# A two-layer diffusion trunk on one core: the end of shared products, the queue of the modulation loads, and buffers for S5's tiles

## The chip, the cores and the metric
One of the eight cores of a Trainium2 chip runs the whole program in one launch. The metric is device time in microseconds (us). Engines: TensorE (PE: matrix products; PEld is its weight load), VectorE (DVE), ScalarE (ACT), GpSimd (POOL) and SyncE (SP). SP issues most DMA transfers, POOL some. Each engine runs its own list of instructions in order and waits on semaphores.

## The reference
Two layers (`DEPTH` 2) over 512 latent tokens and 256 context tokens of width 1024, all in float32:

```
mod = silu(c) @ w_mod[l] + b_mod[l]          # 6 x 1024 values per stream: shift, scale, gate, twice
h   = rmsnorm(x) * (1 + scale) + shift       # latent with c, context with c_ctx
y   = token_mixing(h @ w_in[l])              # S5 | neighbourhood attention | gated linear attention | windowed attention
x   = x + gate * rmsnorm(y @ w_out[l])
h   = rmsnorm(x) * (1 + scale2) + shift2
x   = x + gate2 * rmsnorm((gelu(conv3(h @ w_up_gate)) * (h @ w_up_val)) @ w_down[l])
```

In the last layer the context stream is not updated after the input projection. The output is the latent stream.

## The kernel before
Activations lie with channels on the partitions: H is eight tiles (k = 0 to 7) of 128 channels x 768 tokens, each split into a high part h and a remainder l. Weights are split too: `weights` (line 448) loads 128 x 1024 floats into `wst` (2 buffers) on SP's queue, ACT casts them to `whi`, DVE subtracts to get `wlo` (`split`, lines 268 and 269; four buffers each). A product is then three matmuls: whi x h, whi x l, wlo x h.

`dense4` (line 506) forms several output tiles at once, four of them or six, with four or six weights held. It walks the quarters of tokens (context 512 to 767, then 0 to 255, then 256 to 511), in a quarter the eight k, and for each k all tiles j. It is called four times: at the start of layer 0 (`start`, with the k in two halves), for the first four tiles of layer 1's input projection (`mixing`), and at the start of each layer's FFN (`ffn_start`; four tiles in layer 0, six in layer 1). Its tiles hold the PSUM buffers with the tags m (four) and d (two). After it come single products: `dense` (line 468) in the FFN, `dense_steps` (line 479) in the projections.

Work that can run beside others is written as Python generators: `tails` (the ends of rows: norm, residual, transposes L412, next input L285), `fill` (projections that fill PE's time), `later` (modulation). `step_tail` advances the tails; `gap` advances `fill` by one step, the tails by two, and `later` by `rate` steps. `rate` is `r00` in layer 0's gated linear attention (GLA) stage and `r01` (1) in its S5 stage. There are 18 gaps in the GLA stage. A planner then orders each engine's instructions by the order in which the code issues them (weights ahead of their place) and by a modelled time of when each is ready.

Modulation: in layer 0 `mod_first` forms the first third, and `mod_round` the other two, in 64 steps: each loads 128 x 512 of `w_mod` into `wm` on POOL's queue (L209), then four matmuls (L212; eight records, two passes each). Layer 1's is formed by `mod_sums` during layer 0's FFN: 96 loads on SP's queue (L185), each followed by a multiply-add on DVE (L188, L190; two for the first 32), then matmuls with ones (L195). During the same FFN `s5_build` makes layer 1's S5 tables on DVE and stores them to `s5ops` in DRAM on POOL's queue (L669, L754, L755).

The tag `wm` has three buffers in a pool. It serves the modulation loads and rows, `xr` (next input), `sg` (gates), and in the S5 stage `s5zz`: each of the eight S5 units copies its result there on ACT (L890) and stores it to DRAM (L894). `rsqrt` (lines 260 to 264) is used in the GLA norm: two ACT instructions and three on DVE, with an intermediate `ru`.

Of the kernel before, what the change touches and what calls it, by code (L numbers as in the profile page):

```python
# [10 lines left out]
FT = mybir.dt.float32  # L11
# [5 lines left out]
OP = mybir.AluOpType  # L17
# [6 lines left out]
KT = 8  # L24
SEQ = 512
# [8 lines left out]
EPS = 1e-6  # L34

RATES = ((2, 0, 2), (1, 0, 2))
KN = dict(build=(1, 1, 1, 2, 1, 1, 1, 1, 2, 1, 1), build1=0, r00=3, r01=1, r02=2, r10=0, r11=3, r12=1, glaA=1, glaB=1, s5=2, s5b=2, na1=0, na2=1, sw1=1, sw2=2, swA=4, pump=6, rows=2, d4=2, ahead=3000, s5n=3, gt=2, six=1, bg=1, wat=(0, 2, 4, 6), wmb=5, go0=12, s5e=4, slow=1, slow0=5, ro1=2, ro2=2)
NEG = -1e30


# [39 lines left out]
class Trunk:  # L80
# [93 lines left out]
    def mod_sums(self, r, streams, pool, tag="o"):  # L174


        nc, L = self.nc, self.L[1]
        if r == 0:
            L["mod"] = self.cst.tile([128, 2, 48], FT, name="mod1")
        p = self.ps("modp", tag)  # L180
        for c in range(4):
            acc = [self.bp.tile([128, 512], FT, name=f"macc{s}", tag=f"macc{s}", bufs=1) for s in range(streams)]
            for k in range(KT):
                w = pool.tile([128, 512], FT, name="wm", tag="wm", bufs=3)
                nc.sync.dma_start(w, self.a["w_mod"][1, 128 * k:128 * (k + 1), 2048 * r + 512 * c:2048 * r + 512 * c + 512])  # L185
                for s, o in enumerate(acc):
                    if k == 0:
                        nc.vector.tensor_scalar(o, w, self.cT[:, k, s:s + 1], None, op0=OP.mult)  # L188
                    else:
                        nc.vector.scalar_tensor_tensor(o, w, self.cT[:, k, s:s + 1], o, op0=OP.mult, op1=OP.add)  # L190
                yield
            for s, o in enumerate(acc):
                for j in range(4):

                    nc.tensor.matmul(p[32 * j:32 * j + 32, 128 * c:128 * c + 128], self.ones[:, s], o[:, 128 * j:128 * j + 128],  # L195
                                     start=(c + s == 0), stop=(s == streams - 1), skip_group_check=True)
        self.mod_end(1, r, p, pool, tag)
# [58 lines left out]
    def rsqrt(self, pool, out, ms, cn, tag="nr"):  # L256
        nc = self.nc
        r0 = pool.tile([128, cn], FT, name="r0", tag=tag + "0", bufs=1)
        u = pool.tile([128, cn], FT, name="ru", tag=tag + "u", bufs=1)
        nc.scalar.activation(r0, ms, AF.Ln, bias=self.eps)  # L260
        nc.scalar.activation(r0, r0, AF.Exp, scale=-0.5)
        nc.vector.scalar_tensor_tensor(u, r0, -0.5, r0, op0=OP.mult, op1=OP.mult)
        nc.vector.scalar_tensor_tensor(u, ms, EPS, u, op0=OP.add, op1=OP.mult)
        nc.vector.scalar_tensor_tensor(out, u, 1.5, r0, op0=OP.add, op1=OP.mult)

    def split(self, src, hi, lo):
        nc = self.nc
# [70 lines left out]
    def rows(self, W, A, ks, Z, c0, src, G, AB, H):  # L338
# [9 lines left out]
        for j in range(2):  # L348
            t = c0 // 128 + j
            for h in range(2):  # L350
# [8 lines left out]
                for z, gr in gates(Z[t])[1 - h]:  # L359
                    nc.vector.tensor_tensor(z, z, gr, op=OP.mult)  # L360
                self.step_tail(KN['rows'])
                yield
# [12 lines left out]
    def row_end(self, Z, xo, ms, c0, js, AB, H):  # L375

        nc = self.nc
        y = self.rstd(ms[:, js[0]:js[-1] + 1])
        for _ in range(KN["ro1"]):
            yield  # L380
# [16 lines left out]
    def next_input(self, Z, ms, c0, AB, H):  # L397

        nc = self.nc
        y = self.rstd(ms)  # L400
        for _ in range(KN["ro2"]):
            yield
# [80 lines left out]
    def dense4(self, ws, H, n, before=None):  # L483


        P = [[self.ps("pd4", "m" if j < 4 else "d")] for j in range(len(ws))]
        if n == NT:
            for j in range(0, len(ws), 2):
                p = self.ps("pd4c", "d")
                for i in range(2):  # L490
                    P[j + i].append(p[:, CTX * i:CTX * i + CTX])
        quarters = [c for c in QUARTERS if c[0] < n]
        for ks in (range(4), range(4, 8)) if before else (range(8),):
            for i, (c0, cn) in enumerate(quarters):
                if before:
                    before(i, ks)
                self.end_tail(c0)
                if c0 == quarters[-1][0]:
                    self.close_after()
                for k in ks:  # L500
                    h, sl = H[k], slice(c0, c0 + cn)
                    for j, ((hi, lo), p) in enumerate(zip(ws, P)):

                        o, first = (p[0][:, c0:c0 + cn], c0 == 0) if c0 < SEQ else (p[1], j % 2 == 0)
                        for x, (wt, ht) in enumerate(((hi, h[0]), (hi, h[1]), (lo, h[0]))):
                            self.nc.tensor.matmul(o, wt[:, k, :], ht[:, sl], start=(first and k == 0 and x == 0),  # L506
                                                  stop=(k == KT - 1 and x == 2), skip_group_check=True)
                    self.step_tail(KN['d4'])
        return P

# [2 lines left out]
    def gap(self, n=1):  # L513
        while n and self.fill:
            try:
# [3 lines left out]
                self.fill.pop(0)  # L519
        self.step_tail(KN["gt"])  # L520
        self.pump(self.rate)
# [323 lines left out]
    def s5_unit(self, l, r, U, ops, zd, ctx_out):  # L845

        nc, L, mp = self.nc, self.L[l], self.mp
        lo = 0 if ctx_out else 32
        half = [slice(64 * d, 64 * d + 64) for d in range(2)]
        pa, pb = ops or self.s5_load(l, r)  # L850
        u = [U[2 * r], U[2 * r + 1]]
        p = self.ps("bu", "m")
        for g in range(2):
            for i in range(2):
                for d in range(2):
                    o, c = 96 * (2 * g + i), S_IN + 256 * g + 128 * i + 64 * d
                    nc.tensor.matmul(p[half[d], o:o + 96], pa[:, c:c + 64], u[g][:, 127:31:-1] if d else u[g][:, 0:96], start=True, stop=True)

        rv = pa[:, S_ROT:S_ROT + 576]
        rot = bass.AP(tensor=rv.tensor, offset=rv.offset, ap=[list(rv.ap[0]), [288, 2], [96, 2], [1, 192]])  # L860
        turn = lambda v: v.rearrange("p (d n) -> p d n", d=2)[:, :, None, :].to_broadcast([128, 2, 2, 192])
        x = mp.tile([128, 2, 2, 192], FT, name="s5x", tag="s5x", bufs=2)
        ga = mp.tile([128, 2, 2, 96], FT, name="s5g", tag="s5g", bufs=2)
        sc = mp.tile([128, 384], FT, name="s5s", tag="s5s", bufs=2)
        nc.vector.tensor_tensor(x, turn(p[:, 0:384]), rot, op=OP.mult)
        nc.vector.tensor_tensor(ga, x[:, :, :, 0:96], x[:, :, :, 96:192], op=OP.add)
        for g in range(2):
            dec = L["dec"][:, 2 * r + g:2 * r + g + 1].to_broadcast([128, 96])
            for i in range(2):
                nc.vector.tensor_tensor_scan(sc[:, 192 * g + 96 * i:192 * g + 96 * i + 96], dec, ga[:, g, i], 0.0, op0=OP.mult, op1=OP.add)  # L870
        x = mp.tile([128, 2, 2, 192], FT, name="s5x", tag="s5x", bufs=2)
        nc.vector.tensor_tensor(x, turn(sc), rot, op=OP.mult)

        hh = self.s5h[r % 2]
        xs = [x[half[d]] for d in range(2)]
        f = max(lo, 1)
        nc.vector.tensor_tensor(hh[half[0], :, :, f:96], xs[0][:, :, :, f - 1:95], xs[0][:, :, :, f + 95:191], op=OP.add)
        nc.vector.tensor_tensor(hh[half[1], :, :, 32:96], xs[1][:, :, :, 94:30:-1], xs[1][:, :, :, 190:126:-1], op=OP.add)
        if ctx_out:
            nc.vector.tensor_tensor(hh[half[1], :, :, 0:31], xs[1][:, :, :, 30::-1], xs[1][:, :, :, 126:95:-1], op=OP.add)  # L880
        yield

        py = self.ps("s5o", "m")
        for g in range(2):
            ops = [(pb[:, 512 + 128 * g:640 + 128 * g], u[g][:, lo:96])]
            ops += [(pb[:, 256 * g + 128 * i:256 * g + 128 * i + 128], hh[:, g, i, lo:96]) for i in range(2)]
            for j, (w, m) in enumerate(ops):
                nc.tensor.matmul(py[:, 96 * g + lo:96 * g + 96], w, m, start=(j == 0), stop=(j == len(ops) - 1))  # L888
        z = self.wm.tile([128, 512], FT, name="s5zz", tag="wm", bufs=3)[:, 0:192].rearrange("p (g n) -> p g n", g=2)
        nc.scalar.copy(z[:, :, lo:96], py[:, 0:192].rearrange("p (h n) -> p h n", h=2)[:, :, lo:96])  # L890
        t, m = r // 4, r % 4
        for g in range(2):
            c = 32 * m + 16 * g
            nc.sync.dma_start(zd[t][c:c + 16, :, lo:96].rearrange("c s n -> s c n"), z[:, g, lo:96])  # L894
# [963 lines left out]
```

## Time and profile before

| | us |
|---|---|
| median of 3 runs | 1887.88 |
| the runs | 1888.21, 1887.88, 1882.94 |
| the profiled execution | 1882.5 |
| its span | 1880.7 |
| PE busy | 1773.1 (94%) |
| DVE busy | 1158.3 (62%) |
| ACT busy | 715.3 (38%) |
| POOL busy | 143.8 (8%) |

The span runs from the first instruction to the last. Busy is the time in which an engine executes; DMA issues are not counted in the page's shares. The chain that ended last is PE for 83%. A view by stretch gives each engine's busy time in a stretch and PE's granted clock as a share of 2.4 GHz. In a view in order of time each row has start, duration, engine, line, operation, output<-input, and in brackets the idle time before it and what ended it. Successive matmuls overlap: their pace is the distance of the starts, not the duration.

### The profile page before, as it was taken

Reading aid. Unit: us, or ns where it says so; the run is one execution under the profiler, and the core shown is the slowest. Engines: PE = TensorE matmul, PEld = TensorE weight load, DVE = VectorE, ACT = ScalarE, POOL = GpSimd, SP = SyncE. Lnnn points to the kernel's source line nnn. Section 1 sums busy time; section 2 is a strip of 40 time slices with the busy share of each in tenths; the row PEclk is TensorE's granted clock in tenths of the full one; section 3 lists DMA queues with packets and bytes.
Section 4 is the critical chain, followed back from the end, with each engine's and each line's share of the span. In section 5 each row is a group of like instructions: output and inputs, shape, how many; then the busy total and the mean of one; then the engine's idle time right before and its main releaser. Section 6 shows DMA issues by size and latency. Waiting matters only on the chain.

```text
span 1880.7 us, 30428 instructions
## 1 busy us (share of the span) xinstructions
PE 1773.1 (94%) x11705; PEld 1450.6 (77%) x11705; DVE 1158.3 (62%) x2833; ACT 715.3 (38%) x1476; POOL 143.8 (8%) x270
## 2 busy tenths in 40 slices
PE   4999997889988999999999998999998989999997
PEld 1888676757678888888888888888776788888886
DVE  5696547565778965873772457665764754444446
ACT  4334311355564322222331336642454543323222
POOL 5122221100001010000000000000000000000000
PEclk7999998989999999999999999999999999999999
DMA  9255647402214343542551334234512142323232
GB/s 304 68 161 171 170 136 225 130 1 77 82 57 149 122 142 97 174 159 90 160 166 45 101 88 151 79 102 129 161 51 79 60 128 95 112 82 109 79 112 90
DMA packets 229584, 220.56 MB, mean 117 GB/s; under 512 B 36204, under 2 KB 177958, under 8 KB 229440
## 3 DMA queue, kind: packets, MB, share of 16 engines
q1 hardware_dynamic: 216384, 181.74, 32.1%
q0 software_dynamic: 12768, 36.56, 6.2%
q8 instruction: 92, 1.51, 0.3%
q14 instruction: 52, 0.43, 0.1%
q10 hardware_dynamic: 288, 0.33, 0.1%
HBM read 191.06 MB, written 27.53 MB: 116 GB/s over the span
## 4 chain that ended last, share of the span: by engine, by line
PE 83%; DVE 6%; DMA 5%; ACT 3%; issue 2%; SPq 0%; POOL 0%; DVEq 0%; ACTq 0%; POOLq 0%
PE pd L468 29%; PE pd L306 20%; PE pd L479 13%; PE pd L506 3%; DMA wm<-in_w_mod_dram 3%; PE pd4c L506 2%; PE nao L1047 1%; PE nas L1026 1%; PE s5o L888 1%; PE swo L1159 1%; PE napt L1041 1%; PE go L1274 1%; PE modp L212 1%; PE swpt L1147 1%; DVE wlo L269 1%
## 5 line engine op out<-in xcount | busy, mean ns | idle before, releaser
L269 DVE TENSOR_TENSOR wlo<-wst,whi 128x1024 fp32r<-128x1024 f32 x190 | 232.2, 1222 | 235.4 <-ACT whi L268 230.8
L268 ACT CAST whi<-wst 128x1024 fp32r<-128x1024 f32 x190 | 199.4, 1050 | 431.8 <-PE pd L468 124.9
L306 PE MATMUL pd<-whi,hidh 128*128 128x512 f32 x440 | 171.5, 391 | 0.6 <-DVE za L355 0.6
L306 PE MATMUL pd<-whi,hidl 128*128 128x512 f32 x440 | 171.3, 390 | 0.0
L306 PE MATMUL pd<-wlo,hidh 128*128 128x512 f32 x440 | 170.8, 390 | 0.0
L306 PEld LDWEIGHTS pd<-whi,hidh 128*128 128x128 f32 x440 | 82.6, 188 | 18.8 <-DVE za L355 1.5
L306 PEld LDWEIGHTS pd<-wlo,hidh 128*128 128x128 f32 x440 | 82.6, 188 | 17.5
L306 PEld LDWEIGHTS pd<-whi,hidl 128*128 128x128 f32 x440 | 82.6, 188 | 17.3
L190 DVE SCALAR_TENSOR_TENSOR macc<-wm,cT,macc 128x512 f32<-128x512 f32 x112 | 81.9, 746 | 19.2 <-DMA wm<-in_w_mod_dram 18.9
L1575 DVE TENSOR_TENSOR fg<-fg,pd 128x512 f32<-128x512 f32 x64 | 38.5, 602 | 66.5 <-PE pd L468 64.8
L1574 ACT ACTIVATE fg<-fg 128x512 f32<-128x512 f32 x66 | 36.8, 559 | 105.5 <-DVE fg L1573 99.8
L1625 DVE TENSOR_TENSOR za<-za,pd 128x512 f32<-128x512 f32 (+1 forms) x40 | 21.9, 552 | 71.2 <-PE pd L306 71.2
L1571 ACT ACTIVATE fg<-pd,vb 128x512 f32<-128x512 f32 x64 | 39.4, 617 | 45.3 <-PE pd L468 45.2
L1572 DVE SCALAR_TENSOR_TENSOR fg<-pd,vb,fg 128x511 f32<-128x511 f32 x64 | 42.2, 661 | 15.8 <-ACT fg L1571 15.7
L268 ACT CAST hidh<-fg 128x512 fp32r<-128x512 f32 x66 | 36.1, 547 | 38.6 <-DVE fg L1575 38.3
L468 PE MATMUL pd<-h0h,whi 128*128 128x512 f32 (+1 forms) x118 | 43.0, 365 | 4.7 <-DVE fg L1573 2.9
L468 PE MATMUL pd<-h0h,wlo 128*128 128x512 f32 (+1 forms) x118 | 42.1, 357 | 4.8 <-DVE wlo L269 4.8
L209 POOL DMA_DIRECT2D wm<-in_w_mod_dram x64 | 34.3, 538 | 126.3 <-PE modp L212 81.0
L269 DVE TENSOR_TENSOR hidl<-fg,hidh 128x512 fp32r<-128x512 f32 x66 | 39.2, 597 | 6.9 <-ACT hidh L268 6.9
L1573 DVE SCALAR_TENSOR_TENSOR fg<-pd,vb,fg 128x511 f32<-128x511 f32 x64 | 42.4, 663 | 1.2
L468 PE MATMUL pd<-h1h,whi 128*128 128x512 f32 (+1 forms) x118 | 42.4, 359 | 0.0
L468 PE MATMUL pd<-h2h,whi 128*128 128x512 f32 (+1 forms) x118 | 42.2, 358 | 0.0
(697 smaller groups left out, 5114.3 us busy)
## 6 DMA issues: line engine op xcount, KB each, us to landing
wst<-in_ffn_w_up_dram SPq DMA_DIRECT2D x88, 512.0 KB
wm<-in_w_mod_dram SPq DMA_DIRECT2D x96, 256.0 KB
wst<-in_ffn_w_down_dram SPq DMA_DIRECT2D x44, 512.0 KB
wst<-in_w_in_dram SPq DMA_DIRECT2D x36, 512.0 KB
wm<-in_w_mod_dram POOLq DMA_DIRECT2D x64, 256.0 KB, 3.2
pka<-s5ops SPq DMA_DIRECT2D x16, 544.0 KB
wm<-in_w_mod_dram SPq DMA_DIRECT2D x16, 512.0 KB
wst<-in_w_out_dram SPq DMA_DIRECT2D x12, 512.0 KB
```

What stands on the lines that cost most here:

```text
L190: nc.vector.scalar_tensor_tensor(o, w, self.cT[:, k, s:s + 1], o, op0=OP.mult, op1=OP.add)
L268: nc.scalar.copy(hi, src)
L269: return nc.vector.tensor_tensor(lo, src, hi.bitcast(FT), op=OP.subtract)
L306: self.nc.tensor.matmul(o, ht[:, sl], wp[:, i, :], start=j == 0 and x == 0, stop=j == n - 1 and x == 2)
L468: nc.tensor.matmul(o, wt[:, j, ms], ht[:, c0:c0 + cn], start=j == 0 and i == 0, stop=j == len(ks) - 1 and i == 2)
L479: nc.tensor.matmul(o, wt[:, j, ms], ht[:, c0:c0 + cn], start=j == 0 and i == 0, stop=j == len(ks) - 1 and i == 2)
L506: self.nc.tensor.matmul(o, wt[:, k, :], ht[:, sl], start=(first and k == 0 and x == 0), stop=(k == KT - 1 and x == 2), skip_group_check=True)
L1571: nc.scalar.mul(g, p, cw(1))
L1572: nc.vector.scalar_tensor_tensor(g[:, 1:cn], p[:, 0:cn - 1], cw(0), g[:, 1:cn], op0=OP.mult, op1=OP.add)
L1573: nc.vector.scalar_tensor_tensor(g[:, 0:cn - 1], p[:, 1:cn], cw(2), g[:, 0:cn - 1], op0=OP.mult, op1=OP.add)
L1574: nc.scalar.activation(g, g, AF.Gelu_apprx_tanh)
L1575: nc.vector.tensor_tensor(g, g, p2, op=OP.mult)
```

## The change
In `dense4`, when the last quarter's last four k are reached, the loops are exchanged: all four k of tile 0, then of tile 1, and so on. `step_tail` stands in the merged loop, so it runs for each (k, j). `mod_sums` loads on POOL's queue. `s5zz` becomes a tile of its own tag, with two buffers, in the pool `s5p`, which is open in the GLA and S5 stages. `rsqrt` works in its output tile. `r00` goes from 3 to 4.

```
-KN = dict(... r00=3, ...)
+KN = dict(... r00=4, ...)
...
-                nc.sync.dma_start(w, self.a["w_mod"][1, 128 * k:128 * (k + 1), 2048 * r + 512 * c:2048 * r + 512 * c + 512])
+                nc.gpsimd.dma_start(w, self.a["w_mod"][1, 128 * k:128 * (k + 1), 2048 * r + 512 * c:2048 * r + 512 * c + 512])
...
-        u = pool.tile([128, cn], FT, name="ru", tag=tag + "u", bufs=1)
...
-        nc.vector.scalar_tensor_tensor(u, r0, -0.5, r0, op0=OP.mult, op1=OP.mult)
-        nc.vector.scalar_tensor_tensor(u, ms, EPS, u, op0=OP.add, op1=OP.mult)
-        nc.vector.scalar_tensor_tensor(out, u, 1.5, r0, op0=OP.add, op1=OP.mult)
+        nc.vector.scalar_tensor_tensor(out, r0, -0.5, r0, op0=OP.mult, op1=OP.mult)
+        nc.vector.scalar_tensor_tensor(out, ms, EPS, out, op0=OP.add, op1=OP.mult)
+        nc.vector.scalar_tensor_tensor(out, out, 1.5, r0, op0=OP.add, op1=OP.mult)
...
-                for k in ks:
-                    h, sl = H[k], slice(c0, c0 + cn)
-                    for j, ((hi, lo), p) in enumerate(zip(ws, P)):
-
-                        o, first = (p[0][:, c0:c0 + cn], c0 == 0) if c0 < SEQ else (p[1], j % 2 == 0)
-                        for x, (wt, ht) in enumerate(((hi, h[0]), (hi, h[1]), (lo, h[0]))):
-                            self.nc.tensor.matmul(o, wt[:, k, :], ht[:, sl], start=(first and k == 0 and x == 0),
-                                                  stop=(k == KT - 1 and x == 2), skip_group_check=True)
+                last = 4 if c0 == quarters[-1][0] and ks[-1] == KT - 1 else 0
+
+                order = [(k, j) for k in ks[:len(ks) - last] for j in range(len(ws))]
+                order += [(k, j) for j in range(len(ws)) for k in ks[len(ks) - last:]]
+                sl = slice(c0, c0 + cn)
+                for k, j in order:
+                    h, (hi, lo), p = H[k], ws[j], P[j]
+
+                    o, first = (p[0][:, c0:c0 + cn], c0 == 0) if c0 < SEQ else (p[1], j % 2 == 0)
+                    for x, (wt, ht) in enumerate(((hi, h[0]), (hi, h[1]), (lo, h[0]))):
+                        self.nc.tensor.matmul(o, wt[:, k, :], ht[:, sl], start=(first and k == 0 and x == 0),
+                                              stop=(k == KT - 1 and x == 2), skip_group_check=True)
                     self.step_tail(KN['d4'])
...
-        z = self.wm.tile([128, 512], FT, name="s5zz", tag="wm", bufs=3)[:, 0:192].rearrange("p (g n) -> p g n", g=2)
+        z = self.s5p.tile([128, 2, 96], FT, name="s5zz", tag="s5zz", bufs=2)
```

## Rows read from the trace of the kernel before

**Rows 1.** The page: engine, busy us (share of the span), instructions.
```profile
PE 1773.1 (94%) x11705; PEld 1450.6 (77%) x11705; DVE 1158.3 (62%) x2833; ACT 715.3 (38%) x1476; POOL 143.8 (8%) x270
```
**Rows 2.** By stretch, layer 0's FFN: length, then each engine's busy us, PEclk, DMA.
```profile
600.00:640.00 40.00, 40.00 (x228) 34.96 (x228) 38.85 (x137) 17.54 (x28) 0.00 (x0) 0.97 0.38 116
640.00:680.00 40.00, 40.00 (x233) 34.20 (x232) 38.31 (x90) 10.41 (x17) 4.51 (x6) 1.00 0.60 184
680.00:720.00 40.00, 40.00 (x178) 33.13 (x177) 13.64 (x28) 12.34 (x23) 4.46 (x6) 1.00 0.26 75
```
**Rows 3.** By stretch, around three ends of `dense4`, in S5 and in the GLA stage.
```profile
90.50:95.00 4.50, 1.08 (x6) 0.40 (x4) 4.47 (x22) 3.71 (x9) 0.00 (x0) 0.90 0.01 2
95.00:103.00 8.00, 7.97 (x23) 6.35 (x24) 7.25 (x23) 1.82 (x2) 0.00 (x0) 0.63 0.51 138
...
592.00:599.30 7.30, 0.68 (x4) 0.30 (x2) 7.30 (x14) 2.54 (x5) 0.00 (x0) 0.77 0.68 201
599.30:603.00 3.70, 3.67 (x18) 3.67 (x19) 3.70 (x7) 2.62 (x3) 0.00 (x0) 0.54 0.73 229
...
1537.40:1540.60 3.20, 0.28 (x4) 0.06 (x1) 3.20 (x5) 2.22 (x5) 0.00 (x0) 1.00 0.53 180
1540.60:1545.00 4.40, 4.40 (x13) 3.46 (x14) 3.28 (x6) 3.03 (x4) 0.00 (x0) 0.61 1.07 316
...
332.00:337.00 5.00, 5.00 (x20) 3.71 (x21) 4.77 (x12) 0.00 (x0) 0.54 (x1) 0.55 0.27 82
...
173.00:285.00 112.00, 109.28 (x1348) 79.84 (x1347) 59.18 (x115) 33.95 (x62) 32.29 (x64) 0.98 0.53 158
```
**Rows 4.** PE in order of time: where it waited after `dense4`, and in S5.
```profile
95.03 0.80 PE L479 MATMUL pd<-h0h,wlo 128*128 128x512 f32 x1 [2.97 <-DVE wlo L269]
...
331.93 0.66 PE L212 MATMUL modp<-wm,cT 128*32 128x128 f32 x8 [1.19 <-DMA wm<-in_w_mod_dram]
...
599.34 0.58 PE L468 MATMUL pd<-h0h,wlo 128*128 128x256 f32 x1 [4.83 <-DVE wlo L269]
...
1186.97 0.50 PE L479 MATMUL pd<-h0h,whi 128*128 128x512 f32 x1 [0.70 <-ACT gk L1371]
...
1540.58 0.47 PE L468 MATMUL pd<-h0h,whi 128*128 128x512 f32 x1 [2.92 <-DVE fg L1573]
```
**Rows 5.** The chain that ended last: start, us, what, how many.
```profile
326.70 0.40 PE modp L212 x8
...
1523.05 12.60 PE pd L506 x105
```
**Rows 6.** ACT and DVE in order of time: weights split after `dense4`.
```profile
591.01 1.05 ACT L268 CAST whi<-wst 128x1024 fp32r<-128x1024 f32 x1 [4.29 <-PE pd L506]
...
598.07 1.21 DVE L269 TENSOR_TENSOR wlo<-wst,whi 128x1024 fp32r<-128x1024 f32 x1
...
1535.67 1.05 ACT L268 CAST whi<-wst 128x1024 fp32r<-128x1024 f32 x1 [10.97 <-PE pd L506]
```
**Rows 7.** In order of time: k=4 in a last quarter (PE), and h7l (DVE).
```profile
84.48 0.74 PE L506 MATMUL pd<-h4h,whi 128*128 128x256 f32 x4 [0.21 <-ACT h4h L268]
...
85.62 0.42 DVE L269 TENSOR_TENSOR h7l<-xr,h7h 128x256 fp32r<-128x256 f32 x1
...
586.25 0.28 PE L506 MATMUL pd<-h4h,whi 128*128 128x256 f32 x1
...
586.84 0.42 DVE L269 TENSOR_TENSOR h7l<-xr,h7h 128x256 fp32r<-128x256 f32 x1
```
**Rows 8.** By tile (duration ns min/median/max): POOL's loads, `modp` after 300 us, POOL's stores.
```profile
L209 POOL DMA_DIRECT2D wm<-in_w_mod_dram x64: 536/536/577, 82.7 to 334.7; - x64
DMA to landing us min/median/max: 2.9/3.2/7.1
...
L212 PE MATMUL modp<-wm,cT x56: 272/297/423, 305.5 to 354.9; 128*32 128x128 f32 x56
...
L669 POOL DMA_DIRECT2D s5ops<-E x12: 750/750/786, 650.0 to 694.9; - x12
```

More of the change, by code (lines that the diff above doesn't have):

```diff
@@ L36 @@
 RATES = ((2, 0, 2), (1, 0, 2))
-KN = dict(build=(1, 1, 1, 2, 1, 1, 1, 1, 2, 1, 1), build1=0, r00=3, r01=1, r02=2, r10=0, r11=3, r12=1, glaA=1, glaB=1, s5=2, s5b=2, na1=0, na2=1, sw1=1, sw2=2, swA=4, pump=6, rows=2, d4=2, ahead=3000, s5n=3, gt=2, six=1, bg=1, wat=(0, 2, 4, 6), wmb=5, go0=12, s5e=4, slow=1, slow0=5, ro1=2, ro2=2)
+KN = dict(build=(1, 1, 1, 2, 1, 1, 1, 1, 2, 1, 1), build1=0, r00=4, r01=1, r02=2, r10=0, r11=3, r12=1, glaA=1, glaB=1, s5=2, s5b=2, na1=0, na2=1, sw1=1, sw2=2, swA=4, pump=6, rows=2, d4=2, ahead=3000, s5n=3, gt=2, six=1, bg=1, wat=(0, 2, 4, 6), wmb=5, go0=12, s5e=4, slow=1, slow0=5, ro1=2, ro2=2)
 NEG = -1e30
```

## The prediction
> **What bounds the kernel now.** I read the busy shares first: TensorE (PE) is busy 1773.1 us, 94% of the span of 1880.7 us [rows 1]. So only two things can be taken away: the 107.6 us in which PE has nothing to do, and the stretches in which PE runs at a lower granted clock. Second, the table by stretch: in 600 to 720 us, the middle of layer 0's FFN, PE is busy for all of each 40 us although VectorE (DVE) is at 38.85 and 38.31 of 40 in the first two [rows 2]. There a shorter queue of loads buys nothing. What is left lies at edges between stages. Third, the same table cut finely behind the places where `dense4` ends, because the change reorders these ends [rows 3]: PE idles 4.50 - 1.08 = 3.4 us after the first call (start of layer 0), 7.30 - 0.68 = 6.6 us after layer 0's FFN start, and 3.20 - 0.28 = 2.9 us after layer 1's. Each gap is followed by work at a mean clock of 0.63, 0.54 and 0.61 of full speed, that is partly at 1.2 and partly at 2.4 GHz; before each of them PE had been nearly idle. Time lost to that: 0.37 x 8.0 = 3.0, 0.46 x 3.7 = 1.7, 0.39 x 4.4 = 1.7 us. The fourth call (layer 1's input) leaves one wait of 0.70 us. Fourth, PE's instructions in order of time name the releaser [rows 4]: the split weights (`wlo`) end the first two long gaps, at 95.03 and 599.34 us; an evacuation on DVE (line 1573) ends the one at 1540.58, an evacuation on ScalarE (ACT) the short one.
>
> **Part 1: the last group tile by tile.** A product of 256 columns takes 12.60 / 105 = 0.12 us [rows 5]. Today all tiles of the last quarter close in the last k step: with four weights, the first has its last use 9 products before the end, with six 15. Afterwards 36 and 60. So the first tile and its weight come free 27 x 0.12 = 3.2 us earlier (six weights: 45 x 0.12 = 5.4), the second 18 x 0.12 = 2.2 (36 x 0.12 = 4.3). That is the resource in demand: all four `whi` slots are in use by `dense4`, and the next weight's cast on ACT waits for PE's last use, at 591.01 with 4.29 us of idle before it and at 1535.67 with 10.97 [rows 6]. No product is added.
> - Layer 1's FFN start. 4.3 and 5.4 us both exceed the gap of 2.9, and ACT had been idle for 10.97 us; what DVE does in this gap is the chain itself (`wlo` and the first tiles' convolution). So gap and slow stretch go: 2.9 + 1.7 = 4.6. I take 4.5. What is late next is the second pair's tiles; they are released 4.3 us earlier too.
> - Layer 0's FFN start. The upper bound is 6.6 + 1.7 = 8.3. But DVE is busy for all 7.30 us of this gap [rows 3], with modulation sums, and the `wlo` of 598.07 [rows 6] stood behind those. A cast 2.2 to 3.2 us earlier gives 0 if the planner leaves DVE's order, 3 if it moves with it, 8.3 if the sums step aside. I take 4: three, and half of the clock's loss.
> - Start of layer 0. Upper bound 3.4 + 3.0 = 6.4; DVE is busy 4.47 of 4.50 us of the gap, with the S5 tables too, and 7.25 of the 8.0 after it [rows 3]. I take 2, below half.
> - Layer 1's input: 0.5 of 0.70.
>
> This order wants h7 sooner. The first tile needs it nine products after the first four k steps. At the start there are no such steps left, since the second half of k begins the quarter at 84.48 us: 84.48 + 1.1 = 85.6, and h7l ends at 85.62 + 0.42 = 86.04: 0.5 us of waiting. At layer 0's FFN start k=4 begins at 586.25, so 586.25 + 1.1 = 587.3, and h7l ends at 586.84 + 0.42 = 587.26: just in time [rows 7]. I subtract nothing more than is in the 2 taken at the start. `step_tail` now runs after each (k, j) rather than each k: four to six times as many tail steps are issued early. `end_tail` forces those that this quarter needs in any case, so it changes priorities, no work: 0, within -1 and +1.
> Sum of part 1: 4.5 + 4 + 2 + 0.5 = 11.0 us less (-0.5, the wait for h7l alone, to 20.0).
>
> **Part 2: r00=4 and the S5 tiles.** Of the first layer's 64 modulation steps in `mod_round`, 56 / 8 = 7 run after 300 us, among the S5 units [rows 8]; one costs PE 0.40 us [rows 5], seven 2.8. With 18 gaps before S5, four steps a gap issue all 64 there. In 173 to 285 us PE is busy 109.28 of 112 [rows 3], so the seven lengthen that stage by up to 2.8, and its 2.7 us of idle, partly waits for `wm`, might come once more: 5.5 at worst. In S5 the change saves at best 2.8, the wait of 1.19 us for `wm` at 331.93 [rows 4] and the slow stretch behind it, 0.45 x 5.0 = 2.2 [rows 3]: 6.2. From -3.4 to +5.5; the rows nearest, both PE-bound, cancel, so I take 0. The S5 tiles' own two buffers only take the loads' wait for the S5 stores away, which is inside these bounds; ACT's copy itself waits for PE. `rsqrt` keeps its three DVE instructions and their order: 0.
>
> **Part 3: 96 loads of `mod_sums` from SP's queue to GpSimd's (POOL's).** SP loses 96 issues, POOL gains 96 x 0.54 = 52 us [rows 8]. POOL has room: it is busy 0 and 4.51 us of 40 in 600 to 680. A POOL load lands a median 3.2 us after issue. PE has no idle in 600 to 720 to give back, and at 591 us the weight waits for PE, not for its load, so SP's relief is worth 0. On POOL the loads queue with S5's table stores (`s5ops`), which wait for DVE and ACT, and DVE's sums wait for the loads. Bounds: 0 (no gain, as PE has no idle to give back there) to the 13.2 us of the second rival. I take 0, as these 80 us with DVE nearly full left PE without a gap.
> Twelve of POOL's `s5ops` issues lie at 650 to 695 us, where DVE is nearly full at first, and took 0.750 to 0.786 us each [rows 8]: no issue was stretched. The Trainium skill (SBUF — State Buffer, Summary: rules for kernel authors) speaks against this move: GpSimd's descriptor writing is starved while DVE runs in a mode that takes both shared ports. By that rule the loads would come late, with rival 2's cost from another cause; by the row the term stays 0, and the trace does not agree with the rule for the DVE work of that stretch.
>
> **Sum.** 11.0 - 0 - 0 = 11.0 less. The profiled execution took 1882.5 us, 1.8 beyond its span: 1871.5. Of the three timed runs one is at 1882.94, two at 1887.88 and 1888.21, so the median lies 5.4 above the profile. I expect a like scatter and place the median half-way, 2.5 above the sum: 1874.
>
> **Rivals.**
> 1. The tiles close earlier, but the next product starts when it does now: the engines run lists that the planner ordered by its own times, and DVE is full in two of the three gaps. For it: the `wlo` of 598.07 stood behind other work on a full DVE. Against it: in layer 1 neither sums nor tables run, and ACT stood idle. Then little more than half of layer 1's gap is left, and part 2's loss eats it: 1882.5 - 2 + 1 + 2.5 = 1884.
> 2. Slower: POOL's order. A sum on DVE waits for a load that stands behind a group of stores. Four stores, the issue and the landing are 4 x 0.75 + 0.54 + 3.2 = 6.7 us, two stores 1.5 + 0.54 + 3.2 = 5.2; two groups of each in 640 to 700 give 24. DVE has 80 - 38.85 - 38.31 = 2.8 us free in 600 to 680. PE's cover is the two split weights ahead, 48 products at 40 / 178 = 0.225 us: 10.8. What is beyond it, 13.2, is PE idle, and layer 0's 4 us gain is lost in the same queue: 1882.5 - 7 + 13.2 + 2.5 = 1891. It decides once DVE waits over 10.8 us for `wm` in 640 to 720. Against it: three buffers let a load be issued two sums ahead.
> 3. All bounds are reached: 8.3 + 6.4 + 4.6 + 0.7 + 3.4 = 23.4 less: 1859 + 2.5 = 1862. Against it: DVE full in two gaps.
>
> **How the numbers follow.** The forecast has 0.50, rival 1 0.24, rival 2 0.13, rival 3 0.13. A measurement here tells 0.3%, 5.7 us, from no change; so faster is 0.50 + 0.13 = 0.63 (below 1882.2), the same 0.24, slower 0.13. The forecast's own range is 1868 to 1881; leaving out the ends of rivals 2 and 3, the range is 1863 to 1889.
>
> **What would show it.** Right: after layer 1's FFN start PE idles under 1 us and the clock stays at 1.0; after layer 0's the first `whi` begins about 3 us before `dense4` ends and the gap is 2 to 4 us; no `modp` step of line 212 among S5 units; `wm` on POOL in 580 to 980 with PE still 40.00 of 40. Wrong: a gap as long as now behind `wlo` (rival 1), PE waits in 600 to 1100 (rival 2), or a stage before S5 longer by over 3 us.

## The result and the profile after

The changed kernel takes 1903.30 us (median of 4 runs, 1900.05 to 1906.53), the kernel before beside it 1887.83 (4 runs): a ratio of 1.0086 [1.0062, 1.0111], about 16 us slower, where 1874 was forecast and 1889 was the upper end of the range. The profiled span is 1902.2 us against 1880.7. First the page's busy shares, against [rows 1]:

```profile
PE 1791.1 (94%) x11705; PEld 1465.7 (77%) x11705; DVE 1158.0 (61%) x2833; ACT 726.7 (38%) x1485; POOL 195.5 (10%) x366
```

PE has the same 11705 instructions and is busy 18.0 us longer, so the busy time isn't a fixed amount of work (more in the last section). ACT has nine instructions more. POOL has 96 more, the moved loads. Its busy time is 51.7 us longer, about 96 x 0.54: for POOL the page counts the DMA issues as busy, other than I wrote above.

The table by stretch, of the changed kernel: start of layer 0, the GLA stage, layer 0's FFN start and FFN, layer 1's FFN start (columns as in [rows 2]).

```profile
88.40:93.00 4.60, 2.28 (x19) 1.85 (x17) 4.52 (x22) 4.09 (x9) 0.07 (x1) 1.00 0.01 0
93.00:101.00 8.00, 8.00 (x33) 6.66 (x34) 7.75 (x26) 1.93 (x3) 0.00 (x0) 0.79 0.54 148
...
173.00:306.00 133.00, 124.22 (x1443) 87.64 (x1442) 63.10 (x126) 38.43 (x69) 37.67 (x74) 0.87 0.50 153
...
200.00:240.00 40.00, 34.78 (x423) 22.14 (x423) 15.86 (x33) 7.53 (x13) 13.91 (x29) 0.66 0.46 143
...
606.40:612.60 6.20, 1.58 (x14) 1.38 (x12) 6.20 (x12) 1.31 (x2) 1.07 (x2) 0.95 0.66 205
612.60:616.30 3.70, 3.66 (x17) 3.66 (x18) 3.70 (x9) 2.43 (x3) 0.54 (x1) 0.50 0.66 196
...
640.00:680.00 40.00, 40.00 (x252) 34.42 (x252) 38.24 (x105) 12.00 (x19) 7.85 (x13) 1.00 0.43 135
680.00:720.00 40.00, 40.00 (x189) 33.59 (x189) 26.73 (x75) 10.29 (x17) 9.82 (x15) 1.00 0.50 149
...
1560.80:1564.00 3.20, 3.20 (x29) 3.14 (x28) 2.57 (x4) 2.62 (x3) 0.00 (x0) 1.00 0.84 247
1564.00:1568.40 4.40, 4.40 (x21) 3.64 (x20) 4.10 (x6) 3.56 (x7) 0.00 (x0) 1.00 0.85 256
```

And one line of the same table of the kernel before:

```profile
200.00:240.00 40.00, 39.37 (x458) 27.43 (x455) 26.38 (x43) 18.74 (x34) 12.73 (x26) 1.00 0.52 143
```

What to see: the GLA stage of layer 0, which I had at 98% PE and clock 0.98 [rows 3], now has a stretch of 40 us in which PE idles 5.2 us and gets 0.66 of full speed, between its levels of 1.2 and 2.4 GHz. Layer 1's FFN start has lost its gap altogether; layer 0's keeps most of it. The middle of layer 0's FFN is as before.

Where the 21.5 us of the span came in is read from the first or last product of each stage on PE. These two kernels' rows hold the ends of the GLA stage (first `gds`, last `go`) and the last GLA norm (`gms`) and first product of the neighbourhood attention (NA; `nas`) of layer 1; before:

```profile
184.21 1.32 PE L1241 MATMUL gds<-gv,gke 64*64 64x64 f32 x44
...
287.69 0.33 PE L1277 MATMUL go<-gqd,gS 64*64 64x64 f32 x4
...
1291.19 1.02 PE L1288 MATMUL gms<-gsq,consts 128*128 128x512 f32 x2
...
1343.68 0.70 PE L1026 MATMUL nas<-nk,nq 64*128 64x256 f32 x2
```

after (with two of PE's waits, for later):

```profile
92.99 0.66 PE L478 MATMUL pd<-h0h,wlo 128*128 128x512 f32 x1 [2.32 <-DVE wlo L268]
...
186.69 0.44 PE L1244 MATMUL gds<-gv,gke 64*64 64x64 f32 x6
...
308.61 0.48 PE L1280 MATMUL go<-gqd,gS 64*64 64x64 f32 x4
...
612.64 0.58 PE L467 MATMUL pd<-h0h,wlo 128*128 128x256 f32 x1 [4.66 <-DVE wlo L268]
...
1306.13 1.02 PE L1291 MATMUL gms<-gsq,consts 128*128 128x512 f32 x2
...
1368.40 1.78 PE L1029 MATMUL nas<-nk,nq 64*128 64x256 f32 x8
```

The GLA stage was 287.69 - 184.21 = 103.5 us long and is 308.61 - 186.69 = 121.9. Layer 1's S5 stage (last GLA norm to first NA product) was 52.5 and is 62.3. The same points of four kernels, as differences to the kernel before in us (the last three are no_rate, no_s5buf and dense_pool of the next section; SWA is the windowed attention):

| point on PE | before | after | without r00=4 | without S5's tiles | without both |
|---|---|---|---|---|---|
| first `gds`, layer 0 | 184.2 | +2.5 | +0.9 | +2.4 | -0.3 |
| last `go`, layer 0 | 287.7 | +20.9 | +0.8 | +20.4 | -0.5 |
| first NA product, layer 0 | 368.0 | +16.6 | +4.6 | +18.9 | +0.1 |
| last NA product, layer 0 | 438.5 | +15.0 | +3.4 | +17.6 | -0.7 |
| last SWA product, layer 0 | 544.4 | +15.5 | +3.8 | +10.3 | -7.9 |
| first `dense4` product, layer 1 | 1139.5 | +14.5 | +2.8 | +12.1 | -6.2 |
| last GLA norm, layer 1 | 1291.2 | +14.9 | +3.4 | +10.3 | -7.6 |
| first NA product, layer 1 | 1343.7 | +24.7 | +8.7 | +11.7 | -7.6 |
| last SWA product, layer 1 | 1481.4 | +26.3 | +10.5 | +13.9 | -6.1 |
| last product (its end) | 1869.9 | +21.5 | +4.5 | +8.1 | -10.5 |

One profile of a kernel is good to some 4 us and more: the dense change alone, profiled twice, ended at -6.7 and at -2.5. A single stage can differ by 6 us: pool_only (next section) has the same order on PE, DVE, ACT and POOL as the kernel before until past the GLA stage, and that stage is 109.5 us long in its profile, against 103.5. The 18.4 us are well beyond that, and every kernel with r00=4 and three buffers has them (121.5 to 124.4 us; with r00=3 101.9 to 109.5).

### The profile page after: what moved, and what is told of

The parts are those of the page before. It is cut to its first block, busy times and chain, and to the rows that moved or that the text cites. A ratio compares the mean times of both kernels' runs of the same rounds, so it can differ in the third digit from the quotient of the medians.

```text
span 1902.2 us, 30414 instructions
## 1 busy us (share of the span) xinstructions
PE 1791.1 (94%) x11705; PEld 1465.7 (77%) x11705; DVE 1158.0 (61%) x2833; ACT 726.7 (38%) x1485; POOL 195.5 (10%) x366
## 4 chain that ended last, share of the span: by engine, by line
PE 81%; DVE 6%; DMA 5%; ACT 3%; issue 3%; POOL 1%; SPq 1%; DVEq 0%; ACTq 0%; POOLq 0%
PE pd L467 29%; PE pd L305 20%; PE pd L478 13%; PE pd L509 3%; DMA wm<-in_w_mod_dram 3%; PE pd4c L509 1%; PE nas L1029 1%; PE nao L1050 1%; PE s5o L891 1%; PE modp L212 1%; PE go L1277 1%; PE napt L1044 1%; PE swo L1162 1%; PE swpt L1150 1%; DVE wlo L268 1%
## 5 line engine op out<-in xcount | busy, mean ns | idle before, releaser
L190 DVE SCALAR_TENSOR_TENSOR macc<-wm,cT,macc 128x512 f32<-128x512 f32 x112 | 82.3, 744 | 14.3 <-DMA wm<-in_w_mod_dram 13.9
L185 POOL DMA_DIRECT2D wm<-in_w_mod_dram x96 | 51.8, 540 | 266.2 <-DVE macc L188 121.6
L1575 DVE SCALAR_TENSOR_TENSOR fg<-pd,vb,fg 128x511 f32<-128x511 f32 x64 | 42.2, 659 | 16.6 <-ACT fg L1574 16.6
L209 POOL DMA_DIRECT2D wm<-in_w_mod_dram x64 | 34.3, 538 | 92.9 <-PE modp L212 83.4
L467 PE MATMUL pd<-h0l,whi 128*128 128x512 f32 (+1 forms) x118 | 42.3, 358 | 0.0
```

The costliest lines, as they stand in the source:

```text
L185: nc.gpsimd.dma_start(w, self.a["w_mod"][1, 128 * k:128 * (k + 1), 2048 * r + 512 * c:2048 * r + 512 * c + 512])
L467: nc.tensor.matmul(o, wt[:, j, ms], ht[:, c0:c0 + cn], start=j == 0 and i == 0, stop=j == len(ks) - 1 and i == 2)
L1575: nc.vector.scalar_tensor_tensor(g[:, 1:cn], p[:, 0:cn - 1], cw(0), g[:, 1:cn], op0=OP.mult, op1=OP.add)
```

## The experiments

**The parts one at a time**, each alone on the kernel before. The edits are the hunks of the change: `r00=4`; `mod_sums`' loads on GpSimd's queue; S5's tile with `rsqrt` in place; `dense4`'s order.

- rate_only: 

> The kernel before with only r00=4. Buffer theory with a share for the rate: the modulation steps bunch in layer 0's GLA stage and lengthen it, 1885 to 1892; ScalarE's table loads as before. Rival (rate is neutral alone; only together with the S5 buffers does it cost): 1880 to 1885.

 Measured 1896.26 us, 1.0047 [1.0024, 1.0071].
- s5buf_only: 

> The kernel before with only the S5 tiles' own buffers and rsqrt in place. Buffer theory: slower, about 1892, all of it in layer 1 between its GLA stage and its attention: the planned list of ScalarE has four more table loads there (1.28 us each) and the gates of L1303 among the GLA norms. Rival (the buffers are neutral, the loss is elsewhere): 1880 to 1885.

 Measured 1891.22, 1.0034 [1.0016, 1.0052].
- pool_only: 

> The kernel before with only the 96 loads of mod_sums on GpSimd's queue. Buffer theory: no change, 1879 to 1886. Rival (GpSimd's queue holds the loads back behind the S5 table stores): 1890 or more, with TensorE waits between 600 and 1100 us.

 Measured 1887.64, 1.0008 [0.9992, 1.0024].
- dense_only: 

> The kernel before with the exchanged loops in dense4 alone. Buffer theory (the loss comes from the S5 tiles' own buffers, which free ScalarE's gates to run among the GLA norms, and from r00=4): faster, about 1873 in the profile against 1882.5, with layer 1's FFN start 4 to 5 us shorter. Rival (the new order wants H too early and stalls TensorE): slower than 1885.

 Measured 1874.13, 0.9948 [0.9931, 0.9966].
- dense_again (the same kernel, beside the last four): 

> The dense change alone, for the comparison on one chip: 1872 to 1877, ratio 0.993 to 0.997.

 Measured 1875.25, 0.9947 [0.9927, 0.9968].

rate_only and pool_only came out 4 and 2 us above their ranges. pool_only's profile, at 1891.05, is even where its rival put it, but PE is busy for 40.00 of 40 us in 640 to 680 and in 680 to 720, and 6.0 us of its excess lie in the GLA stage, long ahead of the moved loads: that is the spread named above. Two parts lose, one is free, one gains. Their sum, +0.37%, is less than the 0.86% of the whole, so the parts were also taken out of the changed kernel:

- no_rate (`r00=3`): 

> The changed kernel with r00 back at 3. The planned list has the extra table loads in layer 1 alone. Buffer theory: 1881 to 1884, the sum of dense4 (-10), the queue (0) and the S5 buffers (+6) alone. Rival (the parts just add up, the rate costs 10 whatever the buffers): 1893.

 Measured 1889.01, 1.0006 [0.9989, 1.0023].
- no_s5buf (`s5zz` back in `wm`): 

> The changed kernel with the S5 tiles back in the shared tag wm (r00=4 stays). No extra table load in either layer. Buffer theory: 1885 to 1889, from dense4 (-10) and the rate (+10). Rival (parts add up): 1897.

 Measured 1889.76, 1.0013 [1.0000, 1.0026].
- dense_pool (both undone): 

> The changed kernel with r00=3 and the S5 tile back in the shared buffers: the dense change, the loads on GpSimd's queue and the Newton step in place. All theories: 1873 to 1878, the dense change's gain whole, 52.5 us in layer 1. If the loads on GpSimd's queue cost something that the single run of them hid, 1878 to 1883.

 Measured 1873.81, 0.9943 [0.9923, 0.9963], the fastest kernel here.

no_rate fell between its two ranges. dense_pool holds the moved loads and `rsqrt` in place beside the dense change, and is as fast as the dense change alone: these two cost nothing. From 0.9943, `r00=4` adds 0.70%, S5's tiles 0.63%, and both 1.43%: on this base they add up. Alone on the kernel before they had cost 0.47 and 0.34%; the intervals leave room for both differences. The stages name a likely reason, a short order of layer 0's SWA stage (below): S5's tiles take it away from the dense change (98.7 us become 106.3), and `r00=4` has it even alone (99.8 against 105.9), which makes it look cheaper there.

**Why r00=4 makes the GLA stage longer.** PE's modulation products and the loads that feed them, in the changed kernel (columns: count, duration in ns min/median/max, first to last start; then idle time of its engine and who waited for it, in us and times):

```profile
L212 PE MATMUL modp<-wm,cT x512: 272/297/423, 174.5 to 300.9; 128*32 128x128 f32 x171
...
  DMA wm<-in_w_mod_dram: 6.3, 6
...
  POOL wm L209: 83.4, 36
```

and in the kernel before:

```profile
L212 PE MATMUL modp<-wm,cT x512: 272/273/423, 173.4 to 354.9; 128*32 128x128 f32 x171
```

512 products are 64 steps. Now all 64 lie in 174.5 to 300.9, (300.9 - 174.5) / 63 = 2.0 us apart. The loads on POOL wait 83.4 us for these products, that is for a free `wm` buffer (81.0 before, so the buffers were scarce there too). Theory L: a step goes round a loop (a buffer comes free, its load is issued and lands, PE comes to it in its own order), and with three buffers the loop allows a step in about 2 us, whatever PE's 0.40 us a step may be. The trace's issues, landings and products give the round, as means over the 58 steps of the changed kernel's stage: 3.6 us from issue to landing, 1.4 until PE comes to it, 0.5 of products, 0.5 until the next issue into that buffer, together 6.0, a third of which is 2.0. Two edits test it. The size of the batch:

```
-KN = dict(..., r00=3, ...)
+KN = dict(..., r00=2, ...)
```

dense_r2: 

> The kernel before with the dense change alone and r00=2, so that 36 rather than 47 modulation steps fall to layer 0's GLA stage. Theory L (the stage goes at the pace of the modulation steps, 2.1 to 2.2 us for each): first to last GLA product 75 to 90 us, against 102.9 with r00=3 and 122 with r00=4; the steps that are left go to the S5 stage, which is bound by VectorE, and the time falls below 1874, to 1860 to 1870, if they find room there. Rival N (at r00=3 the stage is already bound by its own chain, and only a fourth step per gap makes it longer): the stage stays at 100 to 104, and the steps pushed into the later stages leave the time at 1874 to 1880.

 Measured 1881.44, 0.9982 [0.9970, 0.9994]. Its stage (186.16 to 278.23) is 92.1 us long:

```profile
186.16 1.15 PE L1245 MATMUL gds<-gv,gke 64*64 64x64 f32 x38
...
278.23 0.33 PE L1281 MATMUL go<-gqd,gS 64*64 64x64 f32 x4
```

Neither range was met: the stage is shorter, as L says, but by less than in proportion (30 steps lie in it, 3.1 us apart), so at r00=2 something else paces it too. The 10.8 us are lost again where the steps go: its last NA product of layer 0 is 5.8 us later than before. The other two kernels have one buffer more, `wx`, for every fourth load, and `s5zz` back in `wm`:

```
-            w = pool.tile([128, 512], FT, name="wm", tag="wm", bufs=3)
+            pl, tg, nb = (self.mp, "wx", 1) if pool is getattr(self, "wm", None) and i % 4 == 3 else (pool, "wm", 3)
+            w = pl.tile([128, 512], FT, name="wm", tag=tg, bufs=nb)
```

four_bufs_r4: 

> The changed kernel with S5's tile back in the shared buffers (as in the run that measured 1889.8 and a GLA stage of 121.5 us), r00=4, and every fourth modulation load into a buffer of its own, so that four loads rather than three can be under way. Theory L (three buffers in a loop of issue, landing and product pace the steps): the steps go at 1.6 to 1.8 us, the GLA stage falls from 121.5 to 95 to 108, and the time by 8 to 15, to 1875 to 1882. Rival P (the steps are paced by TensorE's order or by the DMA queues' bandwidth, not by buffers): the stage stays within 117 to 124 and the time at 1886 to 1892.

 Measured 1877.97, 0.9970 [0.9960, 0.9981].

```profile
L213 PE MATMUL modp<-wm,cT x512: 272/273/423, 172.3 to 280.3; 128*32 128x128 f32 x171
```

```profile
183.94 1.32 PE L1245 MATMUL gds<-gv,gke 64*64 64x64 f32 x44
...
294.29 0.33 PE L1281 MATMUL go<-gqd,gS 64*64 64x64 f32 x4
```

Same work, same r00=4, one buffer more than no_s5buf: steps (280.3 - 172.3) / 63 = 1.7 us apart, the stage 110.4 instead of 121.5 us, and 0.43% off the time. That is L: a buffer's round is now 3.7 + 2.1 + 0.5 + 0.7 = 7.0 us, a quarter of which is 1.75. 110.4 is a little over the range given; the stage still holds 56 steps, where r00=3 has 46 or 47.

four_bufs_r3: 

> The kernel with the dense change alone (1874.1, GLA stage 102.9), r00=3, the third Newton tile left out to make room, and every fourth modulation load into a buffer of its own. Theory L: the stage falls to 80 to 92 and the time to 1862 to 1870. Rival P: the stage stays at 100 to 104, the time at 1872 to 1877.

 Measured 1876.72, 0.9959 [0.9944, 0.9975]: the stage falls from 102.9 to 94.0 us, less than L had, and the time is that of the dense change alone. The stage from the last `go` to layer 0's first NA product is longer by as much (93.2 against 84.9): at r00=3 too the buffers hold the GLA stage up, and what is won there waits in the S5 stage.

An obvious rival is PE's clock: where PE waits, its granted clock falls (last section), and slow products could be what makes the stage long. The lengths don't follow it. In 200 to 240 us the clock is 0.66, 0.70 and 0.83 in the changed kernel, no_s5buf and rate_only, and their stages are 121.9, 121.5 and 124.4 us; it is 1.00 in the kernel before and 0.83 in dense_pool, with stages of 103.5 and 103.3.

**Why S5's own buffers cost.** In the changed kernel, ACT in order of time (start, us, line, what), first layer 0 and then layer 1, with the one cast that [rows 6] showed:

```profile
299.45 0.63 ACT L1306 ACTIVATE sg<-gr 128x512 f32<-128x512 f32 x1
...
306.46 1.28 ACT L259 ACT_TABLE_LOAD   x1
307.75 0.69 ACT L259 ACTIVATE r<-gms,eps 128x512 f32<-128x512 f32 x1
308.46 1.28 ACT L260 ACT_TABLE_LOAD   x1
...
604.18 1.05 ACT L267 CAST whi<-wst 128x1024 fp32r<-128x1024 f32 x1 [1.89 <-PE pd L509]
...
1360.29 0.27 ACT L893 COPY s5zz<-s5o 128x128 f32<-128x128 f32 x1 [2.15 <-PE s5o L891]
```

In the kernel before:

```profile
346.28 0.33 ACT L890 COPY s5zz<-s5o 128x192 f32<-128x192 f32 x1
...
357.10 0.94 ACT L1303 ACTIVATE sg<-gr 128x512 f32<-128x512 f32 x2
```

The gates' Tanh (line 1306, 1303 in the kernel before; tiles `sg`) stood behind the last S5 unit before, at 357.10 and 1339.74 us, although the program asks for nothing like it: `sg` and `s5zz` shared the tag `wm`, whose buffers go round in program order. With `s5zz` gone from there, the planner draws the gates forward to 299 us, ahead of the last GLA norm, whose Ln and Exp then each load their table again (1.28 us). The first theory was these table loads. Holding the Tanh behind the norms (`self.lastexp` is the Exp of `rsqrt`) takes them away:

```
-                    nc.scalar.activation(th, r[:, sl], AF.Tanh, scale=0.5)
+                    with self.tc.issue_after(self.lastexp.ins):
+                        nc.scalar.activation(th, r[:, sl], AF.Tanh, scale=0.5)
```

gates_held: 

> The changed kernel, with one order added: the gates' tanh of L1306 is issued after the last Exp of the GLA norms on ScalarE; buffers, queue, rate and dense4 stay as changed. The planned list has the tables of the kernel before again, eight loads fewer. Buffer theory (the gates among the norms, with their table loads, are the cost of the S5 buffers): 1887 to 1891, that is dense4's -10 and the rate's +10 on the kernel before. Rival (the buffers cost in another way, for instance memory or DMA): within 4 of the changed kernel's 1903.

 Measured 1898.86, 1.0066 [1.0032, 1.0101].

gates_held_r3: 

> The changed kernel with the gates held as before and r00 back at 3. Buffer theory: nothing slow is left, so dense4's gain alone, 1873 to 1878. Rival (the S5 buffers cost more than the tables): 1882 or more.

 Measured 1889.82, 1.0019 [1.0003, 1.0035], against 1.0006 of the same kernel with free gates. The loads were gone and the time was not: that theory fell. The gates still ran among the S5 units. So they were held behind the last unit (`self.lastz` is the copy of its `s5zz`):

```
-                    nc.scalar.activation(th, r[:, sl], AF.Tanh, scale=0.5)
+                    with self.tc.issue_after(self.lastz.ins):
+                        nc.scalar.activation(th, r[:, sl], AF.Tanh, scale=0.5)
```

gates_last (r00=3): 

> The changed kernel with r00=3, and the gates' Tanh (line 1306) issued only behind the copy that ends the last S5 unit. Theory G (the gates, let forward among the S5 units by the freed buffers, delay the units): in layer 1 the first NA product comes back to about 52 us behind the last GLA norm (57.8 in the kernel with r00=3 and free gates, 61.3 in the one with the gates held behind the norms), in layer 0 some 5 us also come back, and the time is near that of the kernel with the dense change alone, 1873 to 1879. Rival T (something else in the two new tiles delays the units, such as the order of loads and zz stores on SyncE): the length stays at 57 to 62 and the time at 1885 to 1892.

 Measured 1881.29, 0.9981 [0.9966, 0.9997]. Half right: layer 0 has its 6 us back (first NA product -1.4 against +4.6; zz_kept and zz_kept_last below repeat it), layer 1's stretch stayed at 57.5. What layer 1 waits for is seen in two rows: VectorE's waits in gates_held_r3 (us, times, longest), and the first copy for NA in the changed kernel.

```profile
DVE nvw L1003 <- DMA s5zd<-s5zz: 6.6, 1, 6.6
```

```profile
1363.57 0.90 DVE L1003 COPY nvw<-nv 128x256 f32<-128x256 f32 x4 [0.61 <-DMA s5zd<-s5zz]
```

NA's first tiles (`nvw`) wait for the store of S5's last tile, which lands 3.0 us behind the end of the copy that filled it (1360.29 + 0.27). They have no data in common. But `s5zz` now lies in the pool `s5p`, which is closed at the end of the stage, and NA's pool takes over its memory; in `wm`, which stays open, it was in nobody's way. The tiles got a pool that stays open until NA is over:

```
+        self.zp = self.open(f"zz{l}", "right")
         s5p = self.open(f"s5p{l}", "right")
...
-        z = self.s5p.tile([128, 2, 96], FT, name="s5zz", tag="s5zz", bufs=2)
+        z = self.zp[1].tile([128, 2, 96], FT, name="s5zz", tag="s5zz", bufs=2)
...
+        self.close(self.zp)
```

zz_kept (r00=3, gates free): 

> The changed kernel with r00=3, and the S5 tiles' two buffers in a pool of their own that stays open until the NA stage is over, so that no NA tile lies in their memory; the gates are free. Theory M (NA's first copies wait for the stores out of that memory): no wait of the nvw copies for s5zd, and the stretch from the last GLA norm to the first NA product in layer 1 falls from 57.8 to 52 to 54 us; the time falls from 1889 to 1881 to 1885. Theory G (gates that run early are what costs there): the stretch stays at 57 to 58, the time at 1887 to 1891.

 Measured 1886.02, 1.0007 [0.9992, 1.0022].

```profile
1294.32 1.02 PE L1291 MATMUL gms<-gsq,consts 128*128 128x512 f32 x2
...
1348.69 1.13 PE L1029 MATMUL nas<-nk,nq 64*128 64x256 f32 x8
```

```profile
1345.01 0.90 DVE L1003 COPY nvw<-nv 128x256 f32<-128x256 f32 x4 [3.00 <-PE s5o L891]
```

The wait for the store is gone and the stretch is 54.4 instead of 57.8, a little over what theory M had; the time did not follow (1.0006 without this pool): 3.4 us of one stretch are about what these intervals leave open.

zz_kept_last (gates held behind the last unit too): 

> The same with the gates' Tanh issued behind the last S5 unit as well. If both theories hold, each in its place: layer 1's stretch 52 to 54 and layer 0's S5 stage as in gates_last, so 1874 to 1879, as dense_pool. If only G: as gates_last, 1880 to 1883 with 57.5 in layer 1.

 Measured 1878.52, 0.9967 [0.9952, 0.9982]; layer 1's stretch is 52.5, as before the change. So both mechanisms are real in the stages, and together they hold 0.39 of the 0.63% (the gates 0.25 by gates_last, just clear of the intervals; the pool's own share is not clear of them). Both were taken out at r00=3 alone. To dense_pool 0.24% is left; the two differ by 7.2 us in layer 0's SWA stage, which is the next point.

**A gain nobody ordered.** In layer 0's SWA stage PE waits for squares (line 392, of the mixer's output norm) which ACT does ahead of the softmax. PE's waits in that stage before, and in dense_pool:

```profile
PE swpt L1147 <- ACT sq L392: 5.3, 1, 5.3
```

```profile
PE swpt L1150 <- DVE pe L1144: 1.8, 1, 1.8
```

From the last NA product to the last SWA product, the kernel before takes 105.9 us and dense_pool 98.7. All seventeen kernels fall near one of the two: the seven that have the dense change or r00=4 and keep `s5zz` in `wm` have the short stage, the kernel before, pool_only and all eight with S5's own buffers the long one. The planner orders ACT's list by its own times, and a shift elsewhere tips it. What tips it stays open: in zz_kept_last the gates are behind the units again, and the stage is long all the same. No run forces this order by itself, so the rows show it and no experiment does.

## Why the prediction was wrong

**The step that failed is part 2**, "r00=4 and the S5 tiles" at 0, with bounds of -3.4 to +5.5. The changed kernel's GLA stage is 121.9 - 103.5 = 18.4 us longer, and S5 gives back 4.3.
- I priced a step by PE: "the seven lengthen that stage by up to 2.8", seven times 0.40. The stage goes by the loop of three buffers, about 2.0 us a step. My count was also low: 464 products from first `gds` to last `go` now and 368 before are 58 and 46 steps, 12 more. 58 steps at 2.10 us are the 121.9, 46 at 2.25 the 103.5. The profile had what was needed: landing 3.2 [rows 8], which is counted from the issue on, and PE's 0.40 [rows 5] are 3.6 us a round; with three buffers that is 1.2 us a step at the very best, three times my price. (Rival 2's 6.7 and 5.2 add the issue's 0.54 to such a landing and so count it twice.) I read PE at 98% of that stage as "PE-bound". It was not: in four_bufs_r3 one buffer more takes 8.9 us off the stage with the same products.
- "The S5 tiles' own two buffers only take the loads' wait for the S5 stores away" was wrong. They took away an order (the gates behind the units) and put NA behind the stores. Layer 1's stage went from 52.5 to 62.3 us; with the two causes removed at r00=3 it is 52.5 again. Of these 9.8 us some 5 are there at r00=3 too; why there are 4.5 more with r00=4 is open.
- "A stage before S5 longer by over 3 us" was named as what would make it wrong; it was in fact the largest single term.

**Part 1 was right as a sum, by luck, and not by its terms.** Forecast -11.0; dense_only gives 0.52% of 1886 us, 9.8.
- Layer 1's FFN start, -4.5: right. PE is busy 3.20 of 3.20 and 4.40 of 4.40 us at clock 1.00, where [rows 3] had 0.28 of 3.20 and 0.61; last SWA product to end gains 4.8 us (26.3 - 21.5), and 4.3 to 6.3 in the kernels with the dense change and little else.
- Layer 0's FFN start, -4: too much. PE's two waits of 1.83 and 4.83 us became one of 4.66, and the slow stretch behind it is still there at 0.50. The weight was cast 2.4 us sooner (3.6 us ahead of the end of `dense4` instead of 1.2, with 1.89 us of idle ahead of it instead of 4.29 [rows 6]), but the second `wlo` still stands behind sums on DVE: here rival 1 was right. From the last SWA product to the first `dense4` product of layer 1 only 1.0 us is gained, none in dense_pool.
- Start of layer 0, -2: the wait of 2.97 [rows 4] is 2.32, and nothing is left of it at the first `gds` (between -0.3 and +2.5).
- Layer 1's input, -0.5: from its first `dense4` product to the last GLA norm dense_pool gains 1.4 us, the changed kernel nothing (+0.4).
- In their place stands the 7.2 us of layer 0's SWA stage, which I did not foresee, and which the changed kernel, with S5's own buffers, does not get.

**Part 3, at 0, was right**, and rival 2 did not come: PE stays at 40.00 of 40 in 640 to 720, and pool_only is 1.0008. POOL issues 96 loads, 540 ns each on average, against 536 [rows 8]; DVE waits for them 13.9 us in all (18.9 on SP's queue, in the kernel before), 1.2 of these in 640 to 720, where rival 2 needed 10.8:

```profile
L190 DVE SCALAR_TENSOR_TENSOR macc<-wm,cT,macc 128x512 f32<-128x512 f32 x112 | 82.3, 744 | 14.3 <-DMA wm<-in_w_mod_dram 13.9
...
L185 POOL DMA_DIRECT2D wm<-in_w_mod_dram x96 | 51.8, 540 | 266.2 <-DVE macc L188 121.6 <-DVE macc L190 79.0 <-DVE E L567 21.2
```

The Trainium skill (SBUF — State Buffer, Summary: rules for kernel authors) warns that GpSimd's descriptor writing is starved while DVE runs in a mode that takes both shared ports. Nine of these issues lie in 640 to 680, with DVE at 38.24 of 40 us, and took 538 ns on average, and the 96 loads landed a median 3.2 us after issue, as in [rows 8]: nothing was stretched, so the trace again shows nothing of it for this DVE work.

**The range and the chances.** "Slower" had 0.13, all of it on POOL's order. I bounded the cost of more steps by PE's idle time, the resource that was full on the page, and of a changed buffer by the wait that it removes. Both bounds were of the wrong resource.

## What to carry to other kernels

Price a moved step by the loop that feeds it (buffers, landing, the consumer's turn), not by the busiest engine's time for it: a stage with many such steps can go at the loop's pace while that engine looks full. Before a tile gets buffers of its own, ask what the shared ones kept in order, and whose memory the new ones will be under when their pool closes; a tile that a DMA still reads holds up whoever inherits its place. When the planner reorders at every change, take single parts from runs, and compare stages, since a gain of several us may be a change of order elsewhere.

## What the runs showed of the hardware

PE's busy time rose by 18.0 us with not one instruction more. Layer 0's GLA and S5 stages together hold 5.8 of it (174.2 against 168.5 us) and layer 1's S5 stage 5.4, at a mean clock of 0.90 where it had been 1.00. The start up to the first `gds` holds 3.9, though its clock was higher than before (0.95 against 0.92). So a lower clock goes with part of the longer busy time and can't be all of it.

In the GLA stage the clock fell after short waits. The table by stretch, of the changed kernel:

```profile
210.00:220.00 10.00, 7.60 (x122) 5.26 (x120) 8.91 (x17) 3.27 (x7) 2.74 (x6) 0.63 0.72 209
220.00:230.00 10.00, 9.81 (x103) 5.75 (x104) 1.55 (x7) 0.00 (x0) 3.06 (x7) 0.50 0.40 127
230.00:240.00 10.00, 7.38 (x66) 4.05 (x66) 1.69 (x6) 0.60 (x1) 3.46 (x8) 0.50 0.40 126
```

PE idled 2.4 us of the first ten, with no recorded wait over 0.82 us, and ran the next twenty at 1.2 GHz. The idle time of the whole stage rose only from 3.1 to 9.2 us, and its mean clock fell from 0.98 to 0.84. No run changes the waits alone.
